# Two column blocks of an output projection by seven products of halves, on one core of a Trainium2 chip

## The chip, the cores and the metric

The kernel runs on one core of one Trainium2 chip. The metric is the device time of one execution in microseconds (us), smaller is better. A core has five engines with a queue of instructions each: TensorE (PE, matmuls), VectorE (DVE), ScalarE (ACT), GpSimd (POOL) and SyncE (SP, which only starts transfers here). ACT and POOL can start transfers (DMAs) too. "PEld" is PE's loading of the stationary operand.

## The reference, cut to what matters

One layer of a decoder on 512 tokens with 2048 channels, all in float32. Half of the channels pass through a recurrence over the tokens (RWKV-7, 16 heads of 64), the other half through pooling over windows; the two results, multiplied by their gates, are put side by side and projected:

```
h = rms_norm(x, norm_g[i])
z = einsum('btd,dn->btn', h, w_in[i])
...
y_mix = concatenate([y_rwkv, y_pool], axis=-1)
x = x + einsum('btc,cd->btd', y_mix, w_out[i])
gate = sigmoid(einsum('btd,de->bte', x, w_pg[i]) + b_pg[i])
x = x + gate * einsum('btq,qd->btd', p[i], w_ple[i])
...
return rms_norm(x, final_g)
```

The change concerns the line with `w_out`: 512 tokens x 2048 channels times 2048 x 2048 weights.

## The kernel before, in words

**Products in three matmuls.** Each float32 operand is split into a high part (rounded to the matmul's float32r) and a low part (the rest). A product is the sum of high by high, high by low and low by high, so three matmuls each. `wsplit` does it for a tile of weights: a load into a raw tile on SP's queue (L129), a cast to the high part on ACT (L132), a subtraction for the low part on DVE (L133). The pool `wp` has four buffers each for raw, high and low tiles (`raw_...`, `whi_...`, `wlo_...` in the rows; the letters behind say which projection: k, r, v, g of the first projection by head pairs, `o` for the output projection, `wp` for the pooling's map). `split` (L137, L138) does the same for activations.

**Stages.** (1) Load x, normalise it, turn it over (`hhi`, `hlo`). (2) Eight pairs of heads at a time: project with columns of `w_in` (`zk`, `zr`, `zv`, `zg`), then the recurrence in `recur`, with the projections of the next pair and of the pooling half (`zb`) between its steps. Until the end of this stage PE's instructions keep the order of the program (`pin`); elsewhere a scheduler orders each engine's queue by its own estimate of when each instruction's inputs are there. Results go to DRAM as `yd`, one piece of 128 channels at a time. (3) Output projection. (4) Gate projection with `w_pg` and the embedding product. (5) Final norm.

**The output projection.** `load_y` fetches the 16 pieces of `yd` (tiles `yin`, six buffers) and splits them into `yhi` and `ylo`; six are fetched ahead, the others within column block 0. There are four column blocks of EC = 512 columns. In each, `proj` goes over 16 k tiles in the order 8 to 13, 0 to 7, 14, 15 (the order in which pieces of y become ready), loads and splits one 128x512 weight tile, and multiplies it with four tiles of 128 tokens: 16 x 4 x 3 = 192 matmuls per block, collected in four PSUM banks (`acc_o`). DVE then adds the residual, which ACT's queue loads (L995), ACT's queue stores the sum to `x2d`, and `turn` transposes the block on PE (16 transposes, `px2`) and splits it into `x2hi`, `x2lo`, the gate projection's input. `turn` of the last block is put into the gate projection's first block (`aside`).

Of the kernel before, what the change touches and what calls it, by code (L numbers as in the profile page):

```python
# [9 lines left out]
F32 = mybir.dt.float32  # L10
F32R = mybir.dt.float32r
# [4 lines left out]
P = 128  # L16
T = 512
# [11 lines left out]
O_U, O_GP = O_G + DR, O_G + 2 * DR  # L29
KAPPA = math.exp(-0.5)  # L30
CK = 4


@with_exitstack
def trunk_kernel(ctx: ExitStack, tc: tile.TileContext, x, p, norm_g, w_in, mu, w0, w_up, a0, a_up,
# [84 lines left out]
    def dp(o, i):  # L120
        return dprm[:, o + i:o + i + 1]

    hhi = hp.tile([P, KT, T], F32R, name="hhi", tag="ahi")
    hlo = hp.tile([P, KT, T], F32R, name="hlo", tag="alo")


    def wsplit(src, kt, n, nm):
# [277 lines left out]
    def pool_unit(n):  # L405
        g, i = n // 4, n % 2
        win = WINDOWS[g]
        ps = psA.tile([P, T], F32, name=f"zb{n}", tag="acc")
        yield from zcols(ps, f"b{n}")
        if n % 4 < 2:  # L410
            u_ = pp.tile([P, T], F32, name=f"u{n}", tag="u")
            nc.scalar.copy(u_, ps)
            s_ = u_
            w_ = 1
            while w_ < win:
                n_ = pp.tile([P, T], F32, name=f"sw{n}_{w_}", tag="sw")
# [21 lines left out]
        nc.scalar.dma_start(out=yd[NJ + m], in_=sgp)  # L438

    phl, pn = [], []  # L440

# [314 lines left out]
    def recur(j, work, between):  # L756
# [17 lines left out]
        for ch in range(NCH):  # L774
# [42 lines left out]
            if ch % 4 == 3:  # L817
# [53 lines left out]
    HS, HN = 5, 2  # L871
    HP = 1000
    pending = []
    need("k", 0)
    need("r", 0)
    prepare_key(0)
# [35 lines left out]
    yhi = ymp.tile([P, KT, T], F32R, name="yhi")  # L912
    ylo = ymp.tile([P, KT, T], F32R, name="ylo")
    AHEAD = 6

    def load_y(k):
        t_ = ymp.tile([P, T], F32, name=f"yin{k}", tag="yin", bufs=AHEAD)
        nc.scalar.dma_start(out=t_, in_=yd[k])
        split(yhi[:, k, :], ylo[:, k, :], t_)

    for k in order[:AHEAD]:
        load_y(k)
# [1 line left out]
    pin[0] = False  # L924


    x2hi = hp.tile([P, KT, T], F32R, name="x2hi", tag="ahi")
    x2lo = hp.tile([P, KT, T], F32R, name="x2lo", tag="alo")
    x2d = dram.tile([T, D], F32, name="x2d", bufs=1)

    KEEP, LATE = 8, 4
# [8 lines left out]
    def proj(w, hi_, lo_, ec, nm, ks=range(KT), tts=range(NT), keep=None, aside=None):  # L940
        acc = {tt: acc_tile(f"acc_{nm}{ec}_{tt}") for tt in tts}
        for i, k in enumerate(ks):
# [9 lines left out]
            else:  # L952
# [34 lines left out]
    for ec in range(D // EC):  # L987
        es = slice(ec * EC, (ec + 1) * EC)
        acc = proj(w_out, yhi, ylo, ec, "o", order)
        x2 = []  # L990
        for tt in range(NT):
            rows = slice(tt * P, (tt + 1) * P)
            t_ = pp.tile([P, EC], F32, name=f"x2_{ec}_{tt}", tag=("u", "sw")[tt // 2])
            nc.scalar.dma_start(out=t_, in_=x[rows, es])
            nc.vector.tensor_tensor(t_, acc[tt], t_, ALU.add)  # L995
            nc.scalar.dma_start(out=x2d[rows, es], in_=t_)
            x2.append(t_)
        def turn(ec=ec, x2=x2):
            for i in range(EC // P):
                pt = psM.tile([P, T], F32, name=f"px2_{ec}_{i}", tag="m")  # L1000
                for tt in range(NT):
                    nc.tensor.transpose(pt[:, tt * P:(tt + 1) * P], x2[tt][:, i * P:(i + 1) * P], ident)
                hi = split(x2hi[:, 4 * ec + i, :], x2lo[:, 4 * ec + i, :], pt)
            return hi


        if ec < D // EC - 1:
            turn()

    sy.close()  # L1010

# [1 line left out]
    with tc.tile_pool(name="fp", bufs=2) as fp, tc.tile_pool(name="kp_", bufs=1) as kp_:  # L1013
# [92 lines left out]
        for ec in range(LAST):  # L1106
            pre = {}
            vec = vectors(ec)
            acc = proj(w_pg, x2hi, x2lo, ec, "g", aside=turn if ec == 0 else None)
# [71 lines left out]
```

## Time and profile before

| | |
|---|---|
| median of 3 runs | 1097.71 us (1096.88 to 1099.16) |
| the profiled execution | 1097.72 us, span 1095.9 us |
| mean granted TensorE clock | 0.998 |
| PE, DVE, ACT, POOL busy | 98%, 65%, 41%, 7% of the span |
| moved by DMA | 138.56 MB, 126 GB/s over the span |
| column block 0 of the output projection | 728.6 to 772.1 us |
| column blocks 1 and 2 | 772.1 to 863 us |

The page of the profile gives the busy time of each engine, the chain of work that ended last, and groups of instructions as "line engine operation out<-in shape x count | busy us, mean ns | idle time of the engine just before, and what ended it". A row of the timeline is "start us, duration us, engine line operation out<-in shape", with the idle time before it and its releaser in brackets. "SPq" and "ACTq" are the transfers started by an engine's queue: the duration there is that of the issue, not of the transfer, and "x4" in such a row means four issues from that start on. Matmuls are pipelined, so the spacing of their starts is smaller than their duration.

### The profile page before, as it was taken

The page shows a single profiled execution, that of the slowest core. Times are in us where ns is not written, and L with a number is a line of the kernel's source. Part 1 is how long each engine was busy: PE and PEld are TensorE (multiplying, and loading weights), DVE is VectorE, ACT ScalarE, POOL GpSimd, SP SyncE. Part 2 cuts the span into 40 slices and gives each one's busy share as a digit, 9 for nine tenths or more (in the row PEclk, how much of TensorE's full clock was granted, in tenths as well). Part 3 has the DMA queues.
Part 4 walks back from the last instruction along what each step waited for, and adds up shares of the span by engine and source line. Part 5 has one row for each costly group of instructions (what it writes and reads, how often), then busy time and mean ns, then how long its engine had stood idle before and what let it go on. Part 6 is the DMA issues. An engine that isn't in the chain of part 4 may idle for free.

```text
span 1095.9 us, 17196 instructions
## 1 busy us (share of the span) xinstructions
PE 1070.8 (98%) x6060; PEld 877.6 (80%) x6060; DVE 708.2 (65%) x1835; ACT 448.3 (41%) x917; POOL 76.9 (7%) x180
## 2 busy tenths in 40 slices
PE   5999999999999999999999999999999999999996
PEld 4888878887788888788878788888888888888885
DVE  6687867878688679678886956454433424445366
ACT  7633535345335335353343344543222222233337
POOL 2100110110110110100101101000000000000000
PEclk9999999999999999999999999999999999999999
DMA  7433433332423333333334242775534438455534
GB/s 233 116 96 97 111 92 84 96 100 73 120 82 105 104 92 89 96 82 93 91 94 119 79 138 93 232 233 169 172 124 136 167 99 244 137 189 137 181 106 154
DMA packets 178486, 138.56 MB, mean 126 GB/s; under 512 B 34678, under 2 KB 139743, under 8 KB 178399
## 3 DMA queue, kind: packets, MB, share of 16 engines
q1 hardware_dynamic: 157694, 103.89, 32.1%
q10 hardware_dynamic: 20704, 33.56, 9.8%
q8 instruction: 48, 0.79, 0.3%
q14 instruction: 40, 0.32, 0.1%
HBM read 118.02 MB, written 18.87 MB: 125 GB/s over the span
## 4 chain that ended last, share of the span: by engine, by line
PE 86%; DVE 5%; DMA 4%; ACT 3%; issue 1%; SPq 0%; ACTq 0%; DVEq 0%
PE acc_o L157 16%; PE zb L157 14%; PE acc_g L157 14%; PE zv L157 8%; PE zk L157 7%; PE zg L157 7%; PE zr L157 7%; PE py L157 2%; PE pple L157 2%; PE pm L157 1%; PE pu L157 1%; DMA n<-nd 1%; PE pp L157 1%; DMA raw_g<-in_w_pg_dram 1%; PE ps L157 1%
## 5 line engine op out<-in xcount | busy, mean ns | idle before, releaser
L133 DVE TENSOR_TENSOR wlo_g<-raw_g,whi_g 128x512 fp32r<-128x512 f32 x84 | 57.0, 685 | 79.6 <-ACT whi_g L132 76.5
L157 PE MATMUL zb<-hhi,whi_b 128*128 128x512 f32 x256 | 107.0, 418 | 0.0
L133 DVE TENSOR_TENSOR wlo_o<-raw_o,whi_o 128x512 fp32r<-128x512 f32 x64 | 43.9, 690 | 91.4 <-ACT whi_o L132 91.4
L157 PE MATMUL zb<-hhi,wlo_b 128*128 128x512 f32 x256 | 100.5, 393 | 0.0
L157 PE MATMUL acc_o<-whi_o,ylo 128*128 128x512 f32 x256 | 100.2, 391 | 0.0
L157 PE MATMUL acc_o<-whi_o,yhi 128*128 128x512 f32 x256 | 99.9, 390 | 0.0
L157 PE MATMUL zb<-hlo,whi_b 128*128 128x512 f32 x256 | 99.9, 390 | 0.0
L157 PE MATMUL acc_o<-wlo_o,yhi 128*128 128x512 f32 x256 | 99.8, 390 | 0.0
L132 ACT CAST whi_g<-raw_g 128x512 fp32r<-128x512 f32 x84 | 51.9, 620 | 102.7 <-PE acc_g L157 55.4
L157 PE MATMUL acc_g<-whi_g,x2hi 128*128 128x512 f32 x208 | 81.3, 391 | 0.0
L157 PE MATMUL acc_g<-wlo_g,x2hi 128*128 128x512 f32 x208 | 80.9, 389 | 0.0
L157 PE MATMUL acc_g<-whi_g,x2lo 128*128 128x512 f32 x208 | 80.7, 389 | 0.0
L132 ACT CAST whi_o<-raw_o 128x512 fp32r<-128x512 f32 x64 | 39.9, 623 | 97.0 <-PE acc_o L157 96.7
L816 POOL TENSOR_SCALAR s0p<-sbd,pw 64x64 f32<-64x64 f32 x96 | 56.6, 589 | 322.8 <-DVE sbd L809 255.0
L132 ACT CAST whi_b<-raw_b 128x512 fp32r<-128x512 f32 x64 | 39.7, 621 | 86.5 <-PE zv L157 35.4
L133 DVE TENSOR_TENSOR wlo_b<-raw_b,whi_b 128x512 fp32r<-128x512 f32 x64 | 43.8, 685 | 34.2 <-ACT whi_b L132 32.9
L157 PEld LDWEIGHTS zb<-hhi,wlo_b 128*128 128x128 f32 x256 | 48.0, 188 | 11.1
L661 DVE TENSOR_TENSOR xw<-xw,tm 128x60 f32<-128x60 f32 (+24 forms) x248 | 52.1, 210 | 6.8
L157 PEld LDWEIGHTS acc_o<-wlo_o,yhi 128*128 128x128 f32 x256 | 48.1, 188 | 10.3 <-DVE wlo_o L133 0.4
L157 PEld LDWEIGHTS acc_o<-whi_o,yhi 128*128 128x128 f32 x256 | 48.1, 188 | 9.7
L157 PEld LDWEIGHTS acc_o<-whi_o,ylo 128*128 128x128 f32 x256 | 48.1, 188 | 9.8
L157 PEld LDWEIGHTS zb<-hhi,whi_b 128*128 128x128 f32 x256 | 48.2, 188 | 8.5
(285 smaller groups left out, 2550.0 us busy)
## 6 DMA issues: line engine op xcount, KB each, us to landing
raw_b<-in_w_in_dram SPq DMA_DIRECT2D x64, 256.0 KB
raw_o<-in_w_out_dram SPq DMA_DIRECT2D x64, 256.0 KB
raw_g<-in_w_pg_dram SPq DMA_DIRECT2D x64, 256.0 KB
raw_k<-in_w_in_dram SPq DMA_DIRECT2D x32, 256.0 KB
raw_r<-in_w_in_dram SPq DMA_DIRECT2D x32, 256.0 KB
raw_v<-in_w_in_dram SPq DMA_DIRECT2D x32, 256.0 KB
raw_g<-in_w_in_dram SPq DMA_DIRECT2D x32, 256.0 KB
n<-nd SPq DMA_DIRECT2D x16, 256.0 KB
```

The costliest lines, as they stand in the source:

```text
L132: nc.scalar.copy(hi, raw)
L133: nc.vector.tensor_tensor(lo, raw, hi.bitcast(F32), ALU.subtract)
L157: i = nc.tensor.matmul(*a, **k)
L661: nc.vector.tensor_tensor(xw[:, 0:n_, s + 1:32], xw[:, 0:n_, s + 1:32], tm[:, 0:n_, 0:w_], ALU.add)
L816: nc.gpsimd.tensor_scalar(s0p[hc, :], nxt[hc, hc], pcn[hc], None, ALU.mult)
```

## The change

Column blocks 1 and 2 are calculated together by seven products of halves (`seven(1, 2)`): tokens in a left and a right half, k tiles in even and odd ones of a pair, columns in block 1 and block 2. Each product is 8 pairs x 2 token tiles x 3 matmuls; together 336. Blocks 0 and 3 remain as they were, as `block_o`.

- Sums of weights. Products 3, 4, 6 and 7 need the sum or difference of two weight blocks. `sums_of` makes four of them in DRAM (`osum`): for each of four pairs of pairs a copy of one operand from DRAM to DRAM on SP's queue (L476, 512 KB), and an adding DMA of the other on GpSimd's queue (L479, 512 KB), 16 of each. The code draws one copy and one add at each step of the recurrence (`next(adds)`). Product 1's difference is made by DVE out of two raw tiles (L1114).
- Sums of inputs. `sab_sums` makes five differences of token halves per pair within column block 0 (L991, 128x256 each) from the `yin` tiles, and splits those of products 1 and 5 there; those of 6, 7 and 2 are split in the phase before they are needed. The `yin` buffers are kept until then. The tile `sr` for two of the differences uses the one buffer of the tag `sgp`.
- Four phases: products 3 and 4, then 1 and 5, then 6 and 7 into the same PSUM banks as 3 and 4, then 2. Between them DVE combines PSUM banks into c11, c12, c21, c22.
- Residual loads, x2 stores and the recall of block 0's sums (`recalled`) are started by GpSimd. The turns of blocks 0, 1 and 2 come after the seven products.
- `hhi`, `hlo`, `x2hi`, `x2lo` are made in quarters, so that the sums of inputs can use their space.

```diff
@@ sums of weights
+    def sums_of(nm, w, c1, c2):
+        t_ = {m: dram.tile([KT // 2, P, EC], F32, name=f"sum_{nm}{m}", bufs=1) for m in (3, 4, 6, 7)}
...
+            jobs_ = [(m, q, one, two) for q in range(0, KT // 2, 2)
+                     for m, one, two in ((3, (0, c2), (1, c2)), (4, (1, c1), (0, c1)),
+                                         (6, (0, c1), (0, c2)), (7, (1, c1), (1, c2)))]
+            for i in range(len(jobs_) + 3):
+                if i < len(jobs_):
+                    m, q, one, _ = jobs_[i]
+                    nc.sync.dma_start(out=at(m, q), in_=pairs(w, *one, q))
+                if i >= 3:
+                    m, q, _, two = jobs_[i - 3]
+                    nc.gpsimd.dma_start(out=at(m, q), in_=pairs(w, *two, q), accum_op=ALU.add)
+                yield
@@ in recur, at each step
             step()
+            next(adds, None)
@@ sums of inputs
+    def sab_sums(q):
+        a1, a2 = yin.pop(2 * q), yin.pop(2 * q + 1)
...
+        two = pp.tile([P, 2, T // 2], F32, name=f"sr{q}", tag="sgp", bufs=1)
+        sraw[1, q], sraw[5, q] = two[:, 0, :], two[:, 1, :]
+        a11, a21, a12, a22 = a1[:, LH], a1[:, RH], a2[:, LH], a2[:, RH]
+        for m, p_, n_ in ((1, a11, a22), (5, a11, a12), (6, a21, a11), (7, a12, a22), (2, a22, a21)):
+            nc.vector.tensor_tensor(sraw[m, q], p_, n_, ALU.subtract)
+        sab_split(1, q)
+        sab_split(5, q)
@@ in proj
+            if nm == "o" and ec == 0 and i % 2 == 1:
+                sab_sums(k // 2)
@@ the seven products
+        def weights(src, q):
...
+            if not isinstance(src, tuple):
+                return wsplit(src(q).unsqueeze(1), 1, EC, nm)
+            raw = [wp.tile([P, 1, EC], F32, name=f"raw_{nm}{i}", tag="raw") for i in range(2)]
+            for r_, s_ in zip(raw, src):
+                nc.sync.dma_start(out=r_, in_=s_(q).unsqueeze(1))
...
+            tt_(raw[0], raw[0], raw[1], sub)
+            split(wh, wl, raw[0])
...
+        run([(sums(3), own(0, 0), m3, False), (sums(4), own(1, 1), m4, False)], lambda q: sab_split(6, q))
...
+        run([((rows(0, c1), rows(1, c2)), summed(1), m1, False), (rows(1, c2), summed(5), m5, False)],
+            lambda q: sab_split(7, q))
+        for a in two:
+            c11.append(tmp("c11", a))
+            tt_(c11[a], m5[a], res_(c1, a), add)
+            tt_(c12[a], c12[a], m5[a], sub)
+            keep_x2(c2, a, c12[a])
...
+            nc.scalar.copy(t_, m1[a])
...
+            tt_(c11[a], c11[a], t_, add)
+        run([(sums(6), summed(6), m3, True), (sums(7), summed(7), m4, True)], lambda q: sab_split(2, q))
...
+        run([(rows(0, c1), summed(2), m2, False)])
...
+    block_o(0, lambda tt: dict(pool=ymp, tag="cx", bufs=6))
+    x21, x22 = seven(1, 2)
+    turn(0, recalled(0))
+    turn(1, x21)
+    turn(2, x22)
+    x23 = block_o(3, lambda tt: dict(pool=pp, tag=("u", "sw")[tt // 2]))
```

The order on SP, before, where the first head pair's weights are loaded (`raw_k0_2` is quarter 2 of projection k of head pair 0):

```order
L129 DMA raw_k0_2_608<-in_w_in_dram 128x4x128
L129 DMA raw_k0_3_626<-in_w_in_dram 128x4x128
L129 DMA raw_r0_0_632<-in_w_in_dram 128x4x128
L129 DMA raw_r0_1_650<-in_w_in_dram 128x4x128
L129 DMA raw_r0_2_656<-in_w_in_dram 128x4x128
L129 DMA raw_r0_3_674<-in_w_in_dram 128x4x128
```

And after, at the same place (`sum_o3` is the weight sum of product 3):

```order
L144 DMA raw_k0_3_636<-in_w_in_dram 128x4x128
L476 DMA sum_o3_601<-in_w_out_dram 128x2x512
L476 DMA sum_o4_602<-in_w_out_dram 128x2x512
L476 DMA sum_o6_603<-in_w_out_dram 128x2x512
L476 DMA sum_o7_604<-in_w_out_dram 128x2x512
L476 DMA sum_o3_601<-in_w_out_dram 128x2x512
L476 DMA sum_o4_602<-in_w_out_dram 128x2x512
L144 DMA raw_r0_0_642<-in_w_in_dram 128x4x128
L144 DMA raw_r0_1_660<-in_w_in_dram 128x4x128
L144 DMA raw_r0_2_666<-in_w_in_dram 128x4x128
L476 DMA sum_o6_603<-in_w_out_dram 128x2x512
L144 DMA raw_r0_3_684<-in_w_in_dram 128x4x128
```

Six copies stand between the last quarter of k and the first of r; the other ten follow one or two at a time between the loads of r, v and g of the same head pair, the last between the quarters 2 and 3 of g. On POOL, five adds come before the memset of `uaz0`, and eleven later:

```order
L479 DMA sum_o7_604<-in_w_out_dram 128x2x512
L479 DMA sum_o3_601<-in_w_out_dram 128x2x512
L378 MEMSET uaz0_576 64x128
L379 MEMSET uaz1_577 64x128
L381 MEMSET sbd0_572 128x128
```

So the adds are not spread over the recurrence's steps either. On DVE in column block 0, before (`wlo_o0_2`: low part of k tile 2's weights):

```order
L133 TENSOR_TENSOR wlo_o0_2_8296<-raw_o0_2_8293,whi_o0_2_8295 128x512
L138 TENSOR_TENSOR ylo_8023<-yin14_8289,yhi_8022 128x512
L133 TENSOR_TENSOR wlo_o0_3_8318<-raw_o0_3_8315,whi_o0_3_8317 128x512
L138 TENSOR_TENSOR ylo_8023<-yin15_8311,yhi_8022 128x512
L133 TENSOR_TENSOR wlo_o0_4_8336<-raw_o0_4_8333,whi_o0_4_8335 128x512
```

And after (`s6r`, `s7r`, `s2r`, `sr` are the input sums, `sl1` and `sl5` low parts of them):

```order
L148 TENSOR_TENSOR wlo_o0_2_8390<-raw_o0_2_8387,whi_o0_2_8389 128x512
L991 TENSOR_TENSOR s6r1_8198<-yin2_8233 128x256
L991 TENSOR_TENSOR s7r2_8203<-yin3_8249 128x256
L153 TENSOR_TENSOR sl5_8218<-sr6_8307,sh5_8217 128x256
L991 TENSOR_TENSOR s2r2_8204<-yin3_8249,yin2_8233 128x256
L991 TENSOR_TENSOR sr0_8361<-yin0_8177,yin1_8193 128x256 x2
L153 TENSOR_TENSOR ylo_8065<-yin4_8275,yhi_8064 128x512
L153 TENSOR_TENSOR sl1_8214<-sr0_8361,sh1_8213 128x256
L153 TENSOR_TENSOR ylo_8065<-yin5_8297,yhi_8064 128x512
L148 TENSOR_TENSOR wlo_o0_3_8412<-raw_o0_3_8409,whi_o0_3_8411 128x512
```

Between two weight tiles there are nine operations where there was one. On DVE where the phase of products 1 and 5 ends and that of 6 and 7 begins (`seven23` and `seven24` are product 5's banks, `f41` and `f42` the new phase's first two weight tiles):

```order
L148 TENSOR_TENSOR wlo_f41_9080<-raw_f41_9077,whi_f41_9079 128x512
L1167 TENSOR_TENSOR c110_9059<-seven23_8823,x_1_0_9060 128x512
L1168 TENSOR_TENSOR c120_8805<-c120_8805,seven23_8823 128x512
L1173 TENSOR_TENSOR c110_9059<-c110_9059,c220_9065 128x512
L1167 TENSOR_TENSOR c111_9068<-seven24_8824,x_1_1_9069 128x512
L1168 TENSOR_TENSOR c121_8806<-c121_8806,seven24_8824 128x512
L1173 TENSOR_TENSOR c111_9068<-c111_9068,c221_9074 128x512
L148 TENSOR_TENSOR wlo_f42_9092<-raw_f42_9089,whi_f42_9091 128x512
```

Six combinations stand between the two weight tiles, four of which read product 5's banks.

More of the change, by code (lines that the diff above doesn't have):

```diff
@@ L31, with __init__, __getitem__ @@
 CK = 4
+class Quarters:
+    def __init__(self, make):
+        self.make, self.tiles = make, {}
+    def __getitem__(self, key):
+        p_, k, c = key
+        if k // 4 not in self.tiles:
+            self.tiles[k // 4] = self.make(k // 4)
+        return self.tiles[k // 4][p_, k % 4, c]
 @with_exitstack
@@ L121, in dp, with quarters @@
         return dprm[:, o + i:o + i + 1]
-    hhi = hp.tile([P, KT, T], F32R, name="hhi", tag="ahi")
-    hlo = hp.tile([P, KT, T], F32R, name="hlo", tag="alo")
+    def quarters(nm, part):
+        return Quarters(lambda c: hp.tile([P, 4, T], F32R, name=f"{nm}{c}", tag=f"{part}{c}"))
+    hhi, hlo = quarters("hhi", "h"), quarters("hlo", "l")
     def wsplit(src, kt, n, nm):
@@ L873, in trunk_kernel @@
     pending = []
+    osum, adds = sums_of("o", w_out, 1, 2)
     need("k", 0)
@@ L919, in load_y @@
         split(yhi[:, k, :], ylo[:, k, :], t_)
+        yin[k] = t_
     for k in order[:AHEAD]:
@@ L991, in trunk_kernel @@
         for tt in range(NT):
-            rows = slice(tt * P, (tt + 1) * P)
-            t_ = pp.tile([P, EC], F32, name=f"x2_{ec}_{tt}", tag=("u", "sw")[tt // 2])
-            nc.scalar.dma_start(out=t_, in_=x[rows, es])
+            t_ = residual(ec, tt, **tile_of(tt))
             nc.vector.tensor_tensor(t_, acc[tt], t_, ALU.add)
-            nc.scalar.dma_start(out=x2d[rows, es], in_=t_)
+            keep_x2(ec, tt, t_)
             x2.append(t_)
[L998 to L1004, printed above, removed]
@@ new lines, in recalled @@
+    def recalled(ec):
+        res = []
+        for tt in range(NT):
+            t_ = pp.tile([P, EC], F32, name=f"x2t_{ec}_{tt}", tag=("u", "sw")[tt // 2])
+            nc.gpsimd.dma_start(out=t_, in_=x2d[tt * P:(tt + 1) * P, ec * EC:(ec + 1) * EC])
+            res.append(t_)
+        return res
+    block_o(0, lambda tt: dict(pool=ymp, tag="cx", bufs=6))
[4 more added lines that the diff above has]
+    x23 = block_o(3, lambda tt: dict(pool=pp, tag=("u", "sw")[tt // 2]))
```

114 lines of the change are left out of this document (107 added, 7 removed).

## The prediction

> **What bounds the kernel now.** I read the page's busy row, chain and groups first, then the stretch of the output projection in windows and in the timeline.
>
> ```profile
> PE 1070.8 (98%) x6060; PEld 877.6 (80%) x6060; DVE 708.2 (65%) x1835; ACT 448.3 (41%) x917; POOL 76.9 (7%) x180
> PE 86%; DVE 5%; DMA 4%; ACT 3%; issue 1%; SPq 0%; ACTq 0%; DVEq 0%
> L157 PE MATMUL acc_o<-whi_o,ylo 128*128 128x512 f32 x256 | 100.2, 391 | 0.0
> ```
>
> TensorE (PE) is busy 98% of the span and holds 86% of the chain that ended last, and the group of output-projection matmuls (256 of its 768) shows no idle time before it. So the kernel is PE's instruction stream. A product taken away is a gain only while every other engine keeps PE fed. What the removed matmuls are worth is their spacing, not the 0.391 us of their rows:
>
> ```profile
> 783.11 0.39 PE L157 MATMUL acc_o<-whi_o,ylo 128*128 128x512 f32 x1
> 783.34 0.39 PE L157 MATMUL acc_o<-whi_o,yhi 128*128 128x512 f32 x1
> 783.56 0.39 PE L157 MATMUL acc_o<-wlo_o,yhi 128*128 128x512 f32 x1
> ...
> 24.70:76.50 51.80, 51.53 (x282) 44.00 (x284) 38.18 (x76) 29.15 (x60) 2.93 (x11) 1.00 0.38 105
> 728.60:772.10 43.50, 43.50 (x192) 35.75 (x191) 20.62 (x33) 16.40 (x28) 0.00 (x0) 1.00 0.54 177
> 731.70:772.10 40.40, 40.40 (x178) 33.16 (x178) 18.60 (x29) 14.65 (x25) 0.00 (x0) 1.00 0.52 169
> 740.00:750.00 10.00, 10.00 (x45) 8.00 (x44) 7.11 (x12) 7.08 (x13) 0.00 (x0) 1.00 0.78 270
> ```
>
> The columns of a window are its length, then busy time of PE, PEld, DVE, ACT and POOL, the granted clock, the DMA share and GB/s. Column block 0's 192 matmuls take 43.5 us, so 0.2266 us each, with PE never idle; DVE works 20.6 of these 43.5 us.
>
> **Matmuls removed.** Seven products of a quarter size, 7 x 8 pairs x 2 token tiles x 3 = 336 matmuls, replace two blocks of 192: 48 fewer, 48 x 0.2266 = **-10.9 us**. This is all the change can gain. But one split weight tile now feeds 6 matmuls (1.36 us) where it fed 12 (2.72 us), so each weight's load, cast and subtraction has half the time, and the added work is what I cost next.
>
> **Block 0: input sums on DVE.** Five subtractions of 128x256 and the splits of two of them per pair of k tiles are new on DVE.
>
> ```profile
> 719.70 0.43 DVE L133 TENSOR_TENSOR wlo_wp<-raw_wp,whi_wp 128x256 fp32r<-128x256 f32 x1 [1.10 <-ACT whi_wp L132]
> 730.88 0.69 DVE L133 TENSOR_TENSOR wlo_o<-raw_o,whi_o 128x512 fp32r<-128x512 f32 x1
> 731.60 0.33 SPq L129 DMA_DIRECT2D raw_o<-in_w_out_dram  x1
> 734.19 0.33 ACTq L438 DMA_DIRECT2D yd<-sgp  x1
> 771.32 2.48 DVE L995 TENSOR_TENSOR x<-acc_o,x 128x512 f32<-128x512 f32 x4
> ```
>
> Four 128x512 operations back to back take 2.48 us, the last of them 0.69, so one costs (2.48 - 0.69) / 3 = 0.60; a 128x256 one I estimate at 0.60 - (0.69 - 0.43) = 0.34. In the 40.4 us from 731.7, the order gives DVE about 27 of the first (16.2 us) and 67 of the second (22.8 us): 39.0 us of work in 40.4, where 18.6 us stood. Each wlo_o now sits behind input sums, the first `sr` tile needs the buffer of the `sgp` store issued at 734.19, and yin buffers come free only after their sums. Where two wlo_o are late by about 1.1 and 1.9 us, PE waits: **+3**, between 0 (four weight buffers absorb it) and +5 (the store's landing, 3.7 us by the yin rows below, plus two operations).
>
> **Phase m1/m5: the raw buffers.** Per pair, two raw tiles for m1 and one for m5 come on SP. Pool `wp` has four raw buffers, and the second raw tile of each pair gets the buffer which the subtraction of the pair before has just read. So the loop is subtraction, load, subtraction. From a subtraction's start to SP's next issue is 0.72 us (730.88 to 731.60). From issue to the use of 256 KB:
>
> ```profile
> 723.15 0.33 ACTq L918 DMA_DIRECT2D yin<-yd  x1
> 725.86 0.62 ACT L137 CAST yhi<-yin 128x512 fp32r<-128x512 f32 x1 [0.53 <-DMA yin<-yd]
> ...
> 724.29 0.33 ACTq L918 DMA_DIRECT2D yin<-yd  x1
> 727.35 0.62 ACT L137 CAST yhi<-yin 128x512 fp32r<-128x512 f32 x1 [0.35 <-DMA yin<-yd]
> ...
> 725.94 0.33 ACTq L918 DMA_DIRECT2D yin<-yd  x1
> 729.62 0.62 ACT L137 CAST yhi<-yin 128x512 fp32r<-128x512 f32 x1 [1.13 <-DMA yin<-yd]
> ```
>
> These give 2.7, 3.1 and 3.7 us; all three casts waited for their load. I take 3.1, the middle one: a round is 3.8 us, while PE eats a pair in 12 x 0.2266 = 2.72. Seven rounds: 26.6 - 19.0 = 7.6 late, less one pair prepared during the phase before (2.7): **+4.9**, between 7 x 3.4 - 21.7 = +2.1 and 7 x 4.4 - 21.7 = +9.1.
>
> **Boundaries and turns.** After m5, six evictions stand on DVE between the first and second weight of the next phase: 6 x 0.60 = 3.6 us, starting some 0.5 us before PE's new phase, then 0.7 for that weight's own subtraction, which PE wants after 1.36 + 0.23 us: 3.6 - 0.5 + 0.7 - 1.6 = **+2.2** (1 to 3). The other two boundaries have two evictions each, hidden by the first weight but for an estimated **+0.3**. The turns of blocks 0 to 2 now come in a row with 12 casts and 12 subtractions: **+0.5** (0 to 3, one landing, where a recalled tile is late). Phases m3/m4 and m6/m7 need a load per 1.36 us. From a cast to the subtraction of its tile:
>
> ```profile
> 751.01 0.62 ACT L132 CAST whi_o<-raw_o 128x512 fp32r<-128x512 f32 x1 [0.91 <-PE acc_o L157]
> 751.66 0.69 DVE L133 TENSOR_TENSOR wlo_o<-raw_o,whi_o 128x512 fp32r<-128x512 f32 x1 [0.59 <-ACT whi_o L132]
> ```
>
> 0.65 us. Four raw buffers that cycle in 0.72 + 3.1 + 0.65 = 4.5 us bring a tile each 1.1 us: nothing. Residual loads and x2 stores on GpSimd: POOL has no instruction in the windows of block 0 above, and their buffers are asked for a phase ahead: nothing; if they come late the price is in the boundary's upper end.
>
> The stage: -10.9 + 3 + 4.9 + 2.2 + 0.3 + 0.5 = **0.0**.
>
> **Weight sums: 16 copies and 16 adding DMAs.** In the code they are drawn one by one in the recurrence, but nothing they read or write waits for it. On SP all 16 copies now stand between the load of raw_k0's last quarter and that of raw_g0's last, six of them ahead of raw_r0; on POOL five adds stand ahead of the first memset of `uaz`, eleven ahead of the second `xw`, each waiting only for its copy. So about 14 of the adds run there as well.
>
> ```profile
> 20.06 4.60 SPq L129 DMA_DIRECT2D raw_k<-in_w_in_dram  x4
> 34.14 4.31 SPq L129 DMA_DIRECT2D raw_r<-in_w_in_dram  x4
> ...
> 52.00 7.41 SPq L129 DMA_DIRECT2D raw_g<-in_w_in_dram  x4
> ...
> 46.82 0.39 PE L157 MATMUL zr<-hhi,whi_r 128*128 128x512 f32 x1
> 57.70 0.39 PE L157 MATMUL zv<-hhi,whi_v 128*128 128x512 f32 x1
> 69.94 0.39 PE L157 MATMUL zg<-hhi,whi_g 128*128 128x512 f32 x1
> ```
>
> The window from the last raw_k0 issue (20.06 + 4.60 = 24.7) to the time at which raw_g0's last quarter must have landed is 51.8 us: zg starts at 69.94, its last quarter 3 x 12 x 0.2266 = 8.2 us later, less 1.6 us for cast and subtraction, 76.5. By the row shown above the DMA engines work 0.38 of it: 32.1 us are free. Full speed is 270 / 0.78 = 346 GB/s, about 340, so 512 KB are 1.54 us. Copies: 16 x 1.54 = 24.7 us. That alone would fit. Adds at the same price: 14 x 1.54 = 21.6 us. Together 46.3 - 32.1 = 14.2 us too much ahead of a load in the same queue. PE's matmuls here keep program order, so it waits: **+14.2**. [...] An add that costs twice as much, because it reads its destination too, gives 24.7 + 43.1 - 32.1 = +35.7; a copy that does, because both its sides lie in DRAM, 49.3 + 21.6 - 32.1 = +38.8; both together +60. I take the price of any 512 KB for both: the page's two queues move loads on SP and loads mixed with stores on ACT at about one price,
>
> ```profile
> q1 hardware_dynamic: 157694, 103.89, 32.1%
> q10 hardware_dynamic: 20704, 33.56, 9.8%
> ```
>
> 103.89 MB in 32.1% and 33.56 MB in 9.8% of 1095.9 us: 295 and 312 GB/s. So it is not the side that costs, and these are the nearest rows.
>
> [...]
>
> **The sum.** 1097.72 is the profiled execution's own time (its span 1095.9 and 1.8 around it; the runs' median is 1097.71, so nothing to adjust). 1097.7 + 0.0 + 14.2 = **1112**.
>
> **The rivals.** (A) Mine: the early copies and adds hold up the first projections by 6 to 24 us (an add at 1.0 to 2.2 us): 1104 to 1121. Chance 0.43. (B) Transfers with both sides in DRAM are dearer: 24 us or more, at one doubled price +36 to +39, some 1135. [...] Against: the two queues' equal rates. 0.17. (C) Early traffic is hidden, because copies wait their turn and the 32.1 us free hold the 24.7 us of copies, and the adds trail; the output stage nets 0.0: 1098, the same. 0.13. (D) Early traffic hidden, but loads land as slowly as the 3.7 us row, since three loads per 2.72 us (0.77 each) fill 85% of the DMA's time: the m1/m5 loop costs 9.1 instead of 4.9, 1102. 0.09. (E) The other side: hidden early, and raw loads landing as the 2.7 us row does. The loop then costs 2.1, and block 0, whose 39.0 us of DVE work fit in 40.4, costs 1: -10.9 + 1 + 2.1 + 2.2 + 0.8 = -4.8, 1093. It decides below a round of 3.8 us, and only if the first projections don't wait. For it: DVE is idle half of the stage and four weight buffers give slack. 0.18.
>
> The range from 1093 to 1135 reaches E's value and B's; some 2 in 10 lie outside, half of E and half of B; A's own range is 1104 to 1121. About 0.2% (2.2 us) is what a measurement of this kernel can tell from no change: faster is E, 0.18; same C, 0.13; slower A, B and D, 0.69.
>
> **What would show it.** Matmuls of the output projection: 720 instead of 768, spaced 0.2266 where fed. Early: zr, zv or zg start later than 46.82, 57.70, 69.94, with PE waiting for DVE or ACT behind a late raw tile and a DMA share near 0.9 between 25 and 90 us; if they start on time, A and B are wrong. In m1/m5: L1114 waits for DMA, with a gap of about 1.1 us of PE for each pair; if PE runs through, the loop term is wrong. At the phase after it one PE gap of about 2 us behind six evictions. In block 0 PE gaps of 1 to 2 us that end on DVE. What makes the number wrong is above all the price of an add, which no row here shows.

## The result, and the profile after

The changed kernel takes 1147.74 us (median of 4 runs, 1146.78 to 1150.64) against 1097.36 us (4 runs): a ratio of 1.046, 95% interval 1.0437 to 1.0483. Forecast was 1112, with a range up to 1135. It is slower, as forecast, but by 50 us instead of 14.

The page of the changed kernel: busy time, the clock granted to TensorE in 40 slices, the DMA share, one DMA queue (packets, MB, share of 16 engines' span) and the chain that ended last:

```profile
span 1145.4 us, 17526 instructions
PE 1080.7 (94%) x6012; PEld 875.3 (76%) x6012; DVE 762.5 (67%) x1959; ACT 478.6 (42%) x983; POOL 115.2 (10%) x232
PEclk9978999999999999999999999999999999999998
DMA  7999343342343332333333342655767726354534
q0 software_dynamic: 7232, 17.83, 6.5%
PE 71%; DMA 15%; DVE 7%; ACT 4%; issue 2%; SPq 1%; ACTq 0%; DVEq 0%
```

PE fell from 98% busy to 94%, and the chain now has 15% DMA where it had 4%. The DMA share is at 9 in the second to fourth slice, and in the third and fourth the clock falls to 7 and 8. Queue q0, GpSimd's, did not exist before. Where the time went is seen from the first and last starts of groups of matmuls (min, median and max duration in ns, then the first and the last start); two rows of before, then four of after:

```profile
L157 PE MATMUL zb<-hhi,whi_b x256: 389/397/501, 120.1 to 726.8; 128*128 128x512 f32 x128
L157 PE MATMUL acc_g<-whi_g,x2hi x208: 388/389/476, 908.9 to 1061.4; 128*128 128x512 f32 x104
```

```profile
L172 PE MATMUL zb<-hhi,whi_b x256: 387/397/501, 154.8 to 761.2; 128*128 128x512 f32 x128
L172 PE MATMUL acc_o<-whi_o,yhi x128: 388/389/483, 763.3 to 954.0; 128*128 128x512 f32 x128
L172 PE MATMUL seven<-whi_f,sh x80: 387/389/632, 832.7 to 904.1; 128*128 128x512 f32 x80
L172 PE MATMUL acc_g<-whi_g,x2hi x208: 388/389/632, 954.7 to 1110.3; 128*128 128x512 f32 x104
```

| stage | before | after | more |
|---|---|---|---|
| to the first zb (first projections) | 120.1 | 154.8 | +34.7 |
| recurrence, to the output projection | 608.5 | 608.3 | -0.2 |
| output projection (728.6 to 908.9; 763.1 to 954.7) | 180.3 | 191.6 | +11.3 |
| gate projection to the end | 187.0 | 190.7 | +3.7 |

Together 49.5 us, the difference of the spans (1145.4 - 1095.9).

**The first projections.** The windows 24.7 to 76.5 and after (length, busy PE, PEld, DVE, ACT, POOL, clock, DMA share, GB/s), then the transfers between 20 and 110 us by queue:

```profile
24.70:76.50 51.80, 41.84 (x201) 33.52 (x200) 19.21 (x48) 19.14 (x39) 13.97 (x21) 0.90 1.07 261
76.50:128.30 51.80, 37.34 (x163) 29.69 (x164) 28.47 (x54) 14.04 (x26) 6.81 (x6) 0.84 0.85 204
```

```profile
q0 software_dynamic: 4295, 8.31, 51.6%
q1 hardware_dynamic: 14400, 13.38, 48.8%
```

The share went from 0.38 to 1.07, so the engines are full, and the adds alone (q0) took 51.6% of these 90 us: 46.4 us for 16, 2.9 us each. PE's timeline shows the waits, each with its length and releaser in brackets:

```profile
48.79 0.50 PE L172 MATMUL zr<-hhi,whi_r 128*128 128x512 f32 x1 [2.36 <-ACT whi_r L147]
54.85 0.51 PE L172 MATMUL zr<-hhi,whi_r 128*128 128x512 f32 x1 [1.37 <-ACT whi_r L147]
61.84 0.79 PE L172 MATMUL zr<-hhi,whi_r 128*128 128x512 f32 x1 [3.70 <-ACT whi_r L147]
62.43 0.63 PE L172 MATMUL zr<-hlo,whi_r 128*128 128x512 f32 x1
62.86 0.63 PE L172 MATMUL zr<-hhi,wlo_r 128*128 128x512 f32 x1
```

Six waits up to 108.6 us (2.4, 1.4, 3.7, 4.0, 1.6 and 11.1) make 24.1 us. The longest is not a wait for a weight but comes of one all the same. The recurrence's first product `pm` waits for `bk`, which VectorE makes, and there `bk` stands behind `wlo_g` of two late raw tiles (the rows are those of PE, VectorE and ScalarE):

```profile
108.64 3.54 PE L172 MATMUL pm<-ar,bk 64*128 64x128 f32 x32 [11.07 <-DVE bk L644]
101.88 0.69 DVE L148 TENSOR_TENSOR wlo_g<-raw_g,whi_g 128x512 fp32r<-128x512 f32 x1 [4.61 <-ACT whi_g L147]
101.23 0.62 ACT L147 CAST whi_g<-raw_g 128x512 fp32r<-128x512 f32 x1 [7.01 <-DMA raw_g<-in_w_in_dram]
```

The rest shows in the last two rows of the fence before: after a wait of 3.7 us the matmuls come every 0.43 us (62.43 to 62.86) instead of 0.227, for some 5 us. By five-microsecond windows of granted clock, busy time times the missing share of the clock, that is about 8 us more, an estimate; with the waits, 32 of the 34.7 us.

**The output projection.** VectorE's timeline in the phase of products 1 and 5 (L1114 is the difference of product 1's two raw tiles, L1160 and L1161 are the combinations after the phase before):

```profile
834.99 0.69 DVE L1114 TENSOR_TENSOR raw_f<-raw_f,raw_f 128x512 f32<-128x512 f32 x1 [0.83 <-DMA raw_f<-in_w_out_dram]
835.60 0.68 DVE L1161 TENSOR_TENSOR c<-seven,x 128x512 f32<-128x512 f32 x1
836.20 0.68 DVE L1160 TENSOR_TENSOR c<-seven,x 128x512 f32<-128x512 f32 x1
836.80 0.68 DVE L1161 TENSOR_TENSOR c<-seven,x 128x512 f32<-128x512 f32 x1
837.39 0.68 DVE L153 TENSOR_TENSOR wlo_f<-raw_f,whi_f 128x512 fp32r<-128x512 f32 x1
838.86 0.69 DVE L1114 TENSOR_TENSOR raw_f<-raw_f,raw_f 128x512 f32<-128x512 f32 x1 [0.18 <-DMA raw_f<-in_w_out_dram]
...
845.83 0.69 DVE L1114 TENSOR_TENSOR raw_f<-raw_f,raw_f 128x512 f32<-128x512 f32 x1 [0.75 <-DMA raw_f<-in_w_out_dram]
...
850.03 0.69 DVE L1114 TENSOR_TENSOR raw_f<-raw_f,raw_f 128x512 f32<-128x512 f32 x1 [1.46 <-DMA raw_f<-in_w_out_dram]
...
862.37 0.69 DVE L1114 TENSOR_TENSOR raw_f<-raw_f,raw_f 128x512 f32<-128x512 f32 x1 [1.09 <-DMA raw_f<-in_w_out_dram]
...
866.71 0.69 DVE L1167 TENSOR_TENSOR c<-seven,x 128x512 f32<-128x512 f32 x1 [0.62 <-PE seven L172]
```

Every difference of these rows waits for its load, as foreseen, at a round of 3.9 to 7.0 us, mostly 4.2, where PE needs a pair per 2.72. The phase runs from 832.7 to some 866.9 (when product 5's bank is free for L1167): 34.2 us for 96 matmuls that need 21.8. Behind it VectorE makes the six combinations without a pause, then the next weight's low part, for which PE waits:

```profile
870.31 0.68 DVE L148 TENSOR_TENSOR wlo_f<-raw_f,whi_f 128x512 fp32r<-128x512 f32 x1
871.05 0.50 PE L172 MATMUL seven<-wlo_f,sh 128*128 128x512 f32 x1 [1.43 <-DVE wlo_f L148]
896.92 0.50 PE L172 MATMUL seven<-wlo_f,sh 128*128 128x512 f32 x1 [1.13 <-DVE wlo_f L148]
```

The last row is the start of product 2, where six more combinations, those after products 6 and 7, stand ahead of the first low part in the same way (892.59 to 896.18).

**The gate projection.** One wait in the last turn, where before 0.71 us stood, with a granted clock of 0.51 for 3.4 us behind it (968.6 to 972.0):

```profile
967.25 0.66 PE L1080 MATMUL px<-ident,x 128*128 128x128 f32 x4 [2.19 <-DVE x2lo L153]
```

### The profile page after: what moved, and what is told of

Same layout as the page of the kernel before. It is cut to its first block, busy times and chain, and to the rows that moved or that the text cites. A ratio compares the mean times of both kernels' runs of the same rounds, so it can differ in the third digit from the quotient of the medians.

```text
span 1145.4 us, 17526 instructions
## 1 busy us (share of the span) xinstructions
PE 1080.7 (94%) x6012; PEld 875.3 (76%) x6012; DVE 762.5 (67%) x1959; ACT 478.6 (42%) x983; POOL 115.2 (10%) x232
## 4 chain that ended last, share of the span: by engine, by line
PE 71%; DMA 15%; DVE 7%; ACT 4%; issue 2%; SPq 1%; ACTq 0%; DVEq 0%
PE zb L172 14%; PE acc_g L172 13%; PE zg L172 7%; PE zv L172 6%; PE zk L172 6%; PE zr L172 6%; PE acc_o L172 5%; DMA raw_f<-in_w_out_dram 3%; DMA raw_r<-in_w_in_dram 2%; DMA yin<-yd 2%; PE py L172 2%; PE pple L172 2%; DMA raw_f<-sum_o 2%; DMA raw_g<-in_w_pg_dram 2%; PE pm L172 2%
## 5 line engine op out<-in xcount | busy, mean ns | idle before, releaser
L172 PE MATMUL zr<-hhi,whi_r 128*128 128x512 f32 x128 | 55.4, 433 | 7.4 <-ACT whi_r L147 7.4
L172 PE MATMUL zv<-hhi,whi_v 128*128 128x512 f32 x128 | 54.8, 428 | 4.0 <-ACT whi_v L147 4.0
L172 PEld LDWEIGHTS zb<-hhi,wlo_b 128*128 128x128 f32 x256 | 48.0, 188 | 11.1
L701 DVE TENSOR_TENSOR tm<-xw,n 128x60 f32<-128x60 f32 (+10 forms) x240 | 50.6, 211 | 6.4
L172 PEld LDWEIGHTS zb<-hlo,whi_b 128*128 128x128 f32 x256 | 48.3, 189 | 7.9
L172 PE MATMUL zg<-hhi,whi_g 128*128 128x512 f32 x128 | 52.8, 412 | 1.6 <-ACT whi_g L147 1.6
L172 PE MATMUL zk<-hhi,whi_k 128*128 128x512 f32 x128 | 53.2, 415 | 0.0
L172 PE MATMUL acc_o<-wlo_o,yhi 128*128 128x512 f32 x128 | 50.4, 394 | 2.5 <-DVE wlo_o L148 2.5
L172 PE MATMUL zr<-hhi,wlo_r 128*128 128x512 f32 x128 | 52.2, 407 | 0.0
```

What stands on the lines that cost most here:

```text
L172: i = nc.tensor.matmul(*a, **k)
L701: nc.vector.tensor_tensor(tm[:, 0:n_, 0:w_], xin[:, 0:n_, s:s + 1].to_broadcast([P, n_, w_]), nb[s // 16][:, s % 16:s % 16 + 1, s + 1:32]. ...
```

## The experiments

**The sums alone.** Four runs on the first term.

`e1_spread`, the changed kernel with copies and adds tied to the steps of the recurrence:

```diff
-            next(adds, None)
+            with tc.issue_after(sp_[0].ins), tc.issue_after(po_[0].ins):
+                next(adds, None)
```

(`sp_[0]`: the last weight load issued on SP, `po_[0]`: GpSimd's last small product `s0p`.)

> The changed kernel with the 16 copies and 16 adding DMAs tied to the recurrence's steps (each copy behind the weight load last issued in the program, each add behind GpSimd's last small product), so that none lies in the first projections. Theory 1 (the early crowd of transfers holds up zr, zv and zg, 34.7 us): the output stage stays as it is, 1147.7 - 34.7 = 1113 us, with zb starting near 120 us again. Rival (24.7 to 50 us of DMA work are paid wherever they lie, or the adds delay GpSimd's products in the recurrence): 1125 us or more.

Measured 1115.46 us (ratio 1.0177, 1.0144 to 1.021): 32 us less than the changed kernel. zb starts at 120.3. So the early crowd is that term, as theory 1 says, but the transfers are not quite free elsewhere: the output projection starts at 737.5, 9 us late. GpSimd's waits between 140 and 700 us (us in total, times, longest) tell why:

```profile
POOL s0p L862 <- DVE sbd L855: 200.2, 35, 12.7
POOL sum_o L481 <- DMA sum_o<-in_w_out_dram: 93.5, 16, 17.3
```

The second row is the one that counts: the adds stand in GpSimd's queue ahead of the recurrence's `s0p`, and each waits there for a copy issued three steps earlier.

`e2_sums`, the kernel before plus `sums_of` and the two lines that use it, `e3_copies`, the same without the line of the adding DMA, and `e4_plain`, the same with that line changed:

```diff
+    osum, adds = sums_of("o", w_out, 1, 2)
...
+            next(adds, None)
```

```diff
-                    nc.gpsimd.dma_start(out=at(m, q), in_=pairs(w, *two, q), accum_op=ALU.add)
+                    nc.gpsimd.dma_start(out=at(m, q), in_=pairs(w, *two, q))
```

> The kernel before, with nothing of the change but the 16 copies and 16 adding DMAs, whose sums nobody reads; its output stage is the old one. Theory 1: the early price alone, 1097.4 + 34.7 = 1132 us. Rival (the delay of the first projections comes of the other edits, such as the input kept in quarters): 1097 to 1102 us.

> The kernel before with the 16 copies alone, no adds. Theory 1 (a copy costs 1.74 us of all DMA engines by the bytes and shares of the changed kernel's trace, 27.9 us in all, which the free 32.1 us hold): 1097 to 1102 us. Rival (copies ahead of weight loads in one queue are enough, since a load waits for all that stands ahead of it): 1110 us or more.

> The kernel before with 16 copies, and 16 plain copies on GpSimd's queue in the place of the adds (they overwrite instead of adding). Theory 1a (an add is dear because it reads its destination too, 2.9 us against a copy's 1.74): 27.9 + 24.4 - 32.1 = +20, 1117 us. Rival 1b (it is dear because GpSimd's queue issues it, or because it shares the engines with SP's queue): as with the adds, about 1132 us.

Measured 1135.83, 1095.72 and 1118.65 us (one run each; before 1097.11). The sums by themselves cost 39 us, copies alone nothing, and plain copies in place of the adds 21.5. All three are within 4 us of theory 1, and the rivals (other edits, copies ahead of loads in the queue, GpSimd's queue as such) fall. The transfers between 20 and 110 us, of the run with adds and of the one with plain copies in their place:

```profile
q0 software_dynamic: 4292, 8.30, 51.1%
```

```profile
q0 software_dynamic: 2304, 8.39, 26.5%
```

The same bytes by the same queue: 46.0 us with adding, 23.9 without, so 2.87 us and 1.49 us for 512 KB. The number of packets alone is not the reason. Over the whole run the adds are 4352 packets and the plain copies 2304, but the copies on SP's queue are 4352 too (q1 has 162046 packets in `e3_copies` and 157694 before), at 1.65 us each by the next row. The copies alone fill the window of the first projections to 0.89, and PE does not notice (51.5 us busy, as before):

```profile
24.70:76.50 51.80, 51.53 (x284) 44.01 (x285) 37.99 (x76) 29.03 (x59) 2.93 (x11) 1.00 0.89 266
```

That is 0.51 x 51.8 = 26.4 us more than the 0.38 of before, 1.65 us a copy. In the prediction's own formula, 16 x 1.65 + 14 x 2.87 - 32.1 = 34.5 us; the changed kernel lost 34.7. That they agree so closely is luck: the same formula gives 34.5 for `e2_sums`, which lost 38.7, and 16 x 1.65 + 14 x 1.49 - 32.1 = 15.2 for `e4_plain`, which lost 21.5. It is good to some 4 to 6 us. What adding costs by itself is the difference of these two runs, 17.2 us.

**Adds alone in the recurrence.** `e5_adds`: copies stay early, adds behind `po_[0]` only. `e13_recur`: the same in the kernel before.

```diff
-            next(adds, None)
+            with tc.issue_after(po_[0].ins):
+                next(adds, None)
```

> The changed kernel with the copies left where they are (early, between the first weight loads) and only the adds tied to the recurrence's steps, each behind GpSimd's last small product. Theory 1 (copies fit into free DMA time, adds do not; in the run with both spread the recurrence lost some 9 us because GpSimd waited for copies that had only just been issued): 1115 - 8 = 1107 us, the first projections and the recurrence as before, the rest in the output stage. Rival (any add among GpSimd's products holds up the recurrence, by its issue time of 1.1 us each): 1112 us or more.

> The kernel before with the 16 early copies and the 16 adds tied to the recurrence's steps, nobody reading the sums. With the copies alone the time was that of before, so what is above it here is the adds in the recurrence. Theory (GpSimd issues each add in 1.1 us between its small products, and some wait for it): 1.5 to 2.5 us above before, 1099 us. Rival (it comes of the other edits, such as the quarters): the time of before.

Measured 1113.77 us (1.0149, 1.0127 to 1.0171), above what theory 1 asked for and in the range of the rival. The stages speak against the rival: in the trace the first projections and the recurrence are as hoped (the output projection starts at 730.2), so the recurrence gave back 7 of its 9 us. But the output projection took 189.4 us in this run, 3 more than in `e1_spread`, so only 1.7 us are seen in the end. The same kernel before with those transfers took 1099.31 us against 1098.03 (1.0009, 1.0 to 1.0019): some 1 us, at the edge of what can be told, where 1.5 to 2.5 was expected. Copies early and adds late cost next to nothing.

**The phase of products 1 and 5.** `e6_yin` (on `e5_adds`) takes the second raw tile elsewhere, `e7_single` (on `e5_adds`) leaves it and the difference out, so that it calculates something else:

```diff
-            raw = [wp.tile([P, 1, EC], F32, name=f"raw_{nm}{i}", tag="raw") for i in range(2)]
+            raw = [wp.tile([P, 1, EC], F32, name=f"raw_{nm}0", tag="raw"),
+                   ymp.tile([P, EC], F32, name=f"raw_{nm}1", tag="yin", bufs=AHEAD).unsqueeze(1)]
```

```diff
-        run([((rows(0, c1), rows(1, c2)), summed(1), m1, False), ...
+        run([(rows(0, c1), summed(1), m1, False), ...
```

> The run above, and the second raw tile of product 1 taken from two buffers that are free in that phase (of the yin tag) instead of the weights' four raw buffers. Theory 2 (in the phase of products 1 and 5 PE waits for a loop subtraction, load, subtraction through one raw buffer): the phase's gaps, 7.1 us in the run with both spread, go but for about 1: some 6 us less than the run above, 1101 us. Rival (three loads per pair are too many for the DMA engines, or the extra subtraction for VectorE): less than 2 us gained.

> The run with only the adds tied, and product 1 takes one weight tile alone: its second load and the subtraction are left out, so the values are others. Theory 2: the same gain as by more buffers, some 6 us, 1101 us. Rival (transfer rate or VectorE): 6 us here too, but hardly any with more buffers. A third theory (the gaps come from 6 matmuls per weight tile alone): no gain in either.

Measured 1108.38 us (1.011, 1.0087 to 1.0133) and 1100.97 us (one run). More buffers gained 5.4 us, so the loop through one raw buffer is real. Leaving the tile out gained 12.8: its output projection takes 175.8 us, 4.5 less than before, the first of these runs in which some of the 10.9 us shows. So 7 us were left that more buffers alone did not mend. Part of it is seen in `e6_yin`, where one 3.0 us wait replaced the many; SP's issues, then VectorE's first differences (L1117):

```profile
796.74 0.33 SPq L144 DMA_DIRECT2D raw_f<-in_w_out_dram  x1
797.16 6.74 SPq L1115 DMA_DIRECT2D raw_f<-in_w_out_dram  x5
...
801.39 1.35 DVE L1117 TENSOR_TENSOR raw_f<-raw_f,raw_f 128x512 f32<-128x512 f32 x2 [0.32 <-DMA raw_f<-in_w_out_dram]
```

The first pair's second tile is issued at 797.16, behind the loads of the next pair, and lands 4 us later.

**The boundary, and the queue of the residuals.** `e8_evict` (on `e6_yin`) draws the six combinations one by one in the callback of the next phase's weights; `e9_actq` (on `e8_evict`) changes the queue in `residual` and `keep_x2`.

```diff
-        for a in two:
-            c11.append(tmp("c11", a))
-            tt_(c11[a], m5[a], res_(c1, a), add)
...
-        run([(sums(6), ...), (sums(7), ...)], lambda q: sab_split(2, q))
+        def then_(q):
+            sab_split(2, q)
+            next(ev, None)
+        run([(sums(6), ...), (sums(7), ...)], then_)
```

```diff
-        nc.gpsimd.dma_start(out=t_, in_=x[...])
+        nc.scalar.dma_start(out=t_, in_=x[...])
-        nc.gpsimd.dma_start(out=x2d[...], in_=t_)
+        nc.scalar.dma_start(out=x2d[...], in_=t_)
```

(`ev` yields after each of the six combinations.)

> The run with two more raw buffers, and the six combinations of banks after products 1 and 5 drawn one by one between the weights of the next phase instead of ahead of its second weight. Theory 3 (these six hold up that weight's subtraction, a gap of 1.4 to 1.9 us): 1.5 to 2 us less than the run with the buffers alone, about 1099 us. Rival (the gap has another cause, the loads that come late after the phase before): the same time as without.

> The run with buffers and spread combinations, and the residual loads and x2 stores back on ScalarE's queue; the recall of block 0 stays on GpSimd. Theory 4 (the gate projection starts some 3 to 4 us slower in all versions with the change, since the last turn's cast stands on ScalarE behind a transfer's issue that waits for a weight load to land, and this comes of the transfers moved to GpSimd): the 2.7 us gap at the last turn falls to the 0.7 us of before, 1105 us. Rival (the gap comes of the crowd of transfers at the stage's end, whichever queue they stand in): 1107 to 1109 us.

`e8_evict` took 1108.05 us (1.0091, 1.0074 to 1.0109), where 1099 was expected, from a start that was itself 7 us too low. Against `e6_yin` the medians differ by 0.3 us. In the profiled executions the output projection fell from 185.6 to 182.3 us. PE's wait behind the six combinations, in `e6_yin`

```profile
835.22 0.50 PE L172 MATMUL seven<-wlo_f,sh 128*128 128x512 f32 x1 [0.80 <-DVE wlo_f L148]
```

is gone in `e8_evict`, where PE runs without a wait from 823.25 to 840.33. So the combinations were its cause, as theory 3 says, but it was worth 0.8 us there, not 1.5 to 2, and the medians hardly show it.

`e9_actq` took 1103.9 us (1.0051, 1.0035 to 1.0068), 4 less. Of the last turn, the timeline of PE and the waits of ScalarE between 905 and 975 us (us in total, times, longest), in `e8_evict` the first two fences, in `e9_actq` the two behind:

```profile
925.88 1.11 PE L1082 MATMUL px<-ident,x 128*128 128x128 f32 x4 [2.74 <-DVE x2lo L153]
```

```profile
ACT x2hi L152 <- DMA raw_g<-in_w_pg_dram: 5.5, 1, 5.5
```

```profile
923.23 0.65 PE L1082 MATMUL px<-ident,x 128*128 128x128 f32 x4
```

```profile
ACT x2hi L152 <- PE px L1082: 2.5, 1, 2.5
```

With the residual transfers on GpSimd, the cast x2hi came 5.5 us late, by the profile's releaser with a load of w_pg; without, it waits for its transposes alone, and from the gate projection's start to the end 186.3 us pass (190.8 in `e8_evict`, 187.0 before). Theory 4 holds. What stood ahead of the cast is seen on ScalarE, two rows of `e8_evict` and one of `e9_actq`:

```profile
918.45 6.03 ACTq L1312 DMA_DIRECT2D x2r<-x2d  x3
924.52 0.58 ACT L152 CAST x2hi<-px 128x512 fp32r<-128x512 f32 x1 [5.45 <-DMA raw_g<-in_w_pg_dram]
```

```profile
929.50 0.33 ACTq L1312 DMA_DIRECT2D x2r<-x2d  x1
```

Three loads `x2r`, which fetch the stored sums again, stand ahead of the cast there and take 6.03 us to issue. With the stores on ScalarE's queue again, as before, the first `x2r` comes only behind the casts.

**Attempts at the rest.** `e10_pairs` (on `e8_evict`): all copies drawn at the first step, two adds at the end of each head pair, and the first pair of product 1 through the four raw buffers again; `e11_all`: `e10_pairs` and `e9_actq` in one.

```diff
+            if ch == NCH - 2:
+                with tc.issue_after(po_[0].ins):
+                    for _ in range(2):
+                        next(adds, None)
...
+                   wp.tile([P, 1, EC], F32, name=f"raw_{nm}1", tag="raw") if q == QO[0] else
                    ymp.tile([P, EC], F32, name=f"raw_{nm}1", tag="yin", bufs=AHEAD).unsqueeze(1)]
```

> The run with buffers and spread combinations, the adds two at a time at the end of each head pair's recurrence instead of one per step, and the first pair of product 1 loaded through the four raw buffers again, so that its second tile is not issued behind later ones. Theory: the recurrence loses nothing any more (2 us less), and the 3.3 us gap at the start of products 1 and 5 falls below 1: 1103 to 1104 us. Rival (the recurrence's 2 us come of the copies, the gap of the rate of loads): 1107 us or more.

> The two runs above in one. If both theories hold, 1099 to 1101 us, still not below the kernel before, since block 0, the boundaries and the turns keep some 5 us of gaps and 10.9 us are all that 48 matmuls can give. If neither holds, 1107 us.

1108.05 us (1.0093, 1.0078 to 1.0108) and 1106.88 us (1.0082, 1.0059 to 1.0105): misses. The wait at the start of the phase moved to the second pair and grew to 4.0 us, and the recurrence lost a little more, not less (the output projection starts at 732.7 instead of 730.5). From the gate projection's start to the end, `e11_all` takes 186.2 us and `e10_pairs` 190.0, so the change of queue gained there once more.

`e12_spare` (on `e5_adds`, with the edits of `e8_evict` and `e9_actq` but not the `yin` buffers) puts the second raw tiles in the space of product 6's input sums:

```diff
+            n_ = QO.index(q)
+            if n_ % 2 == 0:
+                spare[0] = pp.tile([P, 2, EC], F32, name=f"rs{q}", tag=("dh", "dl")[n_ // 2 % 2], bufs=1)
+            raw = [wp.tile([P, 1, EC], F32, name=f"raw_{nm}0", tag="raw"), spare[0][:, n_ % 2:n_ % 2 + 1, :]]
```

> The run with spread combinations and the residual transfers on ScalarE's queue, and the second raw tiles of product 1 in the space of the input sums of product 6 (tags dh and dl, two tiles each, free from the end of the first phase on), so that four of them are loaded ahead of the phase. Theory (the 3.1 us gap at the phase's start, and the slower clock behind it, come of the first pair's second tile, which stood behind later loads in SP's queue): the gap goes, 1104 - 4 = 1100 us. If nothing else is left but the recurrence's 1.5 us and some ten gaps of 0.2 to 0.9 us, it ends 0 to 3 us above the kernel before. Rival (VectorE is late with the first pair whatever is loaded): 1103 us or more.

1099.05 us (1.0012, 1.0001 to 1.0024) with before at 1098.03: 5 less than `e9_actq`, as the theory said. Four second tiles are loaded ahead, and of the longer waits in the phase one of 2.0 us is left, with the clock granted in full over the stage:

```profile
730.50:909.20 178.70, 173.22 (x772) 139.06 (x771) 120.35 (x225) 80.75 (x154) 2.29 (x4) 1.00 0.64 206
```

The stage takes 178.7 us, 1.6 less than before (180.3): here the seven products gain a little of their 10.9 us.

`e14_bounds` (on `e12_spare`) draws the combinations after the first and third phase between the next weights too, by generators like `ev`:

```diff
-            lambda q: sab_split(7, q))
+            then1_)
...
-        run([(rows(0, c1), summed(2), m2, False)])
+        run([(rows(0, c1), summed(2), m2, False)], lambda q: next(ev3, None))
```

> The run with spare buffers, and the combinations after the first and the third phase drawn between the next phase's weights too. Theory (what is left above the seven products' own time is the two gaps of 2.0 and 1.2 us at those boundaries, behind four and six combinations in a row on VectorE): 2 us less, 1097 us, level with the kernel before or up to 0.2% below it. Rival (the first of these gaps is a late load, the combinations were hidden): 1098 to 1099 us again.

1097.28 us with before at 1097.72: a ratio of 0.9992, 0.998 to 1.0005. This is level with the kernel before, the best of these versions, and no gain that can be told. Its time fits the theory's 2 us, its trace only in part. The wait of 1.2 us at product 2's start is gone. The wait of 2.0 us was, as the rival says, behind a late load: in `e12_spare` a difference waits for it when the four combinations (to 800.85) are long done.

```profile
803.99 0.69 DVE L1119 TENSOR_TENSOR raw_f<-raw_f,rs 128x512 f32<-128x512 f32 x1 [1.94 <-DMA raw_f<-in_w_out_dram]
```

In `e14_bounds` shorter waits stand in their place. PE's waits of 0.15 us or more in the output projection add up to 5.1 us (5.2 in `e12_spare`), and the stage takes 178.2 us in the profiled execution. There it starts at 733.8, 5 us later than before: what the stage gains is lost in the recurrence, which carries the adds. That execution was the slowest of its twelve (1100.05 us).

## Why the prediction was wrong

- **The sign and the reading of what bounds the kernel were right**: PE's stream, 48 matmuls fewer (6012 for 6060), and a price in the first projections, where the order of SP and POOL puts copies and adds. zr, zv and zg started later, behind late raw tiles, at a DMA share near 1.
- **The step that failed first is the price of an add.** I took the price of any 512 KB, 1.54 us, for copies and adds, as "the nearest rows". The copies were near it (1.65), the adds cost 2.87. With these prices the term's formula gives 34.5 instead of 14.2, and 34.7 were measured. The price of adding is some 17 us of that (`e2_sums` against `e4_plain`); with plain copies in place of the adds 21.5 us were lost, 7 more than my term, so the formula itself is some microseconds short. This is rival B, to which I gave 0.17, and its value for a doubled add, +35.7, lies near the 34.7 measured. The argument against it from the equal rates of two queues did not bear on it, since those queues carried loads and stores and no adds. The rival of hidden traffic (C, D, E) fell for the adds; for the copies alone it is what happened. The adds did not trail behind the loads: between 20 and 110 us they took 51.6% of the engines' time and SP's queue 48.8%, and a cast waited 7.01 us for its load (101.23). What an add costs was measured, why was not: that it reads its destination too was my guess and was not shown. The pages of `e2_sums` and `e4_plain` count the same bytes read from HBM, 134.80 MB.
- **The loop of products 1 and 5: +12.4 instead of +4.9**, above even my upper bound of 9.1. The mechanism was right and the size off: rounds of about 4.2 us, one of 7.0, instead of 3.8, and at the start four combinations between the first differences, a boundary for which I had counted two.
- **Block 0: +3 forecast, +3.2 found** (192 matmuls end 3.2 us after their own time), in two waits on DVE's wlo_o of 1.1 and 1.4 us.
- **The boundary behind product 5: +2.2 forecast, a wait of 1.4 found.** The mechanism was right: the six combinations stand ahead of the low part for which PE waits, and in `e8_evict`, where they are spread, there is no such wait. For the other two boundaries I counted two combinations each and put 0.3 on both; the code has four and six, and the six before product 2 made a wait of 1.1 us.
- **What is left of the stage.** -10.9 + 12.4 + 3.2 + 1.4 + 1.1 = 7.2 of the 11.3 us that the output projection lost. The other 4 were not followed to a cause.
- **The transfers moved to GpSimd: "nothing", and it was about 4 us**, not in the stage where I looked but after it, where ScalarE's queue held up a cast. I named what hides the moved transfers in the output projection and not what stands on ScalarE behind it. With the stores gone from that queue, the loads `x2r` stand ahead of the last turn's casts, and their issue takes 6.03 us; why the scheduler puts them there was not traced.
- **The clock: not in the sum at all.** The longer of these waits cost more than their length, an estimated 8 us in the first projections, where windows of five microseconds behind them show a granted clock of 0.50 to 0.82.

## What to carry to other kernels

Before transfers are added to a kernel that is bound by TensorE, sum their engine time against the free DMA time up to the next load that must land, and see from the queues' order, not from the code, where they run: 16 copies were free there, 16 adds behind them cost 39 us, and in the recurrence about 1. An adding DMA counted nearly twice here (2.87 us against 1.49). A saving of matmuls by products of halves halves the time that each weight has (6 matmuls of 0.2266 us, 1.36 us, instead of 12 in 2.72), so look first at how many raw buffers a pair of loads goes through: with spare buffers, the right queue and later adds, the same seven products came from 50 us slower to level, and no further: in the output projection they gained some 2 of 10.9 us, and about as much was lost again in the recurrence, which carries the adds.

## What the runs showed of the hardware

- An adding DMA of 512 KB from DRAM to DRAM took 2.87 us of all 16 engines, a plain one by the same queue 1.49 us, a copy on SP's queue 1.65 us. SP's copies moved in as many packets as the adds, 4352.
- After PE had waited 3.7 us, its matmuls came every 0.43 us instead of 0.227 for some 5 us, and the changed kernel's windows 60 to 65 and 65 to 70 us show it. The first row shows the same behind the wait of 2.4 us (columns as above, the granted clock is the third number from the end):

```profile
50.00:55.00 5.00, 3.63 (x11) 2.33 (x10) 0.17 (x1) 1.69 (x3) 0.00 (x0) 0.66 1.12 212
60.00:65.00 5.00, 3.16 (x8) 2.44 (x9) 0.69 (x1) 1.15 (x3) 2.22 (x2) 0.56 1.09 330
65.00:70.00 5.00, 5.00 (x18) 4.04 (x17) 3.56 (x6) 3.60 (x8) 1.14 (x1) 0.76 1.11 257
```

Behind the wait of 2.4 us the matmuls came every 0.43 us from 50.72 to 52.85. After a wait of 1.4 us (54.85) there was no such stretch: from 55.91 they came every 0.23 us, and the granted clock from 55 to 60 us was 1.00. What sets the clock was not shown.
